# Rotating queries and keys on chip instead of by accumulating transfers

## The chip, the cores and the metric

The kernel runs on one core of a Trainium2 chip. The core has five engines that matter here: PE (TensorE, matrix products), DVE (VectorE), ACT (ScalarE), POOL (GpSimd) and SP (SyncE). Each takes its instructions strictly in the order in which they stand in its own program. PE, DVE and ACT compute; SP issues plain transfers; POOL issues nothing but transfers that add into their destination. All transfers are carried out by 16 DMA engines that the two issuers share. The metric is the device time of one execution in microseconds (us), and the median of several runs is compared.

## The reference

One encoder layer is applied to two sequences, a sample of 1024 tokens and a prompt of 512, with model width 2048. One input projection feeds a convolution group and an attention group of 8 query heads over 2 key and value heads. This work is about one step of it, the rotary embedding of queries and keys:

```python
def apply_rope(t, pos):
    half = HEAD_DIM // 2
    ...
    t1, t2 = tf[..., :half], tf[..., half:]
    out = jnp.concatenate([t1 * cos - t2 * sin, t2 * cos + t1 * sin], axis=-1)

def mixer_layer(x, ...):
    h = rms_norm(x, norm_g)
    z = h @ w_in
    c_val, c_glu, c_gate, q, k, v, a_gate = jnp.split(z, split_points, axis=-1)
    q = apply_rope(q.reshape(B, S, N_HEADS, HEAD_DIM), pos)
    k = apply_rope(k.reshape(B, S, N_KV_HEADS, HEAD_DIM), pos)
    ...
    return x + jnp.concatenate([conv_out, attn_out], axis=-1) @ w_out
```

The head dimension is 128. On the chip a head is stored transposed: the 128 dimensions lie on the 128 partitions and 512 tokens lie along each partition. The halves t1 and t2 are then partitions 0 to 63 and 64 to 127, and an elementwise engine operation does not bring a value from one half to the other unless its output is placed on other partitions than its input.

## The kernel before

**Products in units.** Each float32 operand is split into a high and a low part, and a product of blocks is three matmuls. The sample's projection goes in units: a unit computes two columns of outputs (c = 0, 1) for two halves of the tokens (t = 0, 1) with seven block products P1, P2, P6, P5, P7, P3, P4 of 12 matmuls each, in that order, with sums and differences of the operands (`Unit.product`, L177). The products accumulate in three PSUM banks that PE reuses inside the unit: P1, P6, P7 and P4 follow each other in bank `a`, P5 and P3 in bank `c`, P2 is in `b`. After P1, P6, P5, P7 and P4 the bank's content is copied out by ACT before the next product goes on adding to it (`Unit.tap`, L217); DVE adds the pieces (L237).

**Preparing weights.** For a unit, DVE forms differences of weight blocks (L138), ACT rounds each block to its high part (L438), and DVE forms the low part (L439). The same two engines also carry the taps, the convolution (DVE, L906, one of 31 taps at a time) and the attention.

**Totals.** Each unit runs over half of the inner dimension; the second pass over a column pair adds the first pass's result, which lies in DRAM (`part_q` for queries, `part_kv` for keys and values, `part_gate`, `part_conv`). That addition is an accumulating transfer issued by POOL (`add_into`, L429). What is to be done with a total is a generator that goes into a list; it takes its first step some products later (`turn_over`; `landing` = 4) and one further step at each product after that.

**The rotation.** For queries and keys that step is `rotate` (sample, in units) or `rotated` (prompt, whose jobs leave a complete result in a PSUM bank). DVE multiplies the result once by the table of sines (L932, into a second tile `b`) and once by the table of cosines (L933); SP stores the cosine product to DRAM (`q_d`, `k_d`); POOL then issues two accumulating transfers, which add the two halves of `b` crosswise into what was stored. In the sample the second tile comes from a ring of four tiles named `a`. Attention reads `q_d` and `k_d` from DRAM later.

**What sets the order.** The program is written out once; each engine's order is fixed by a scheduler that estimates times. Tiles come from rings of fixed length: whoever takes a tile waits until the last user of that place in the ring has finished. At the end of the sample's projection (`last_before`, L1719) SP loads the prompt's 16 input blocks (`xr_d`, L1709 into ring `a`, L1706 into ring `p`), and ACT and DVE split each into two parts (L441, L442) between the taps of the last unit.

Of the kernel before, what the change touches and what calls it, by code (L numbers as in the profile page):

```python
# [9 lines left out]
AF = mybir.ActivationFunctionType  # L10
ALU = mybir.AluOpType
PSUM = bass.MemoryType.PSUM

P = 128
# [19 lines left out]
W = 512  # L34
# [619 lines left out]
class Sequence:  # L654
# [270 lines left out]
            nc.vector.tensor_tensor(self.cos, self.cos, self.R, ALU.mult)  # L925
            nc.vector.tensor_tensor(self.sin, self.sin, self.R, ALU.mult)

    def rope(self, acc, c, o, b):

        nc = self.e.nc  # L930
        i = slice(c * W, c * W + W)
        nc.vector.tensor_tensor(b, acc, self.sin[:, i], ALU.mult)  # L932
        nc.vector.tensor_tensor(o, acc, self.cos[:, i], ALU.mult)  # L933

    def rotated(self, dst, accs):
        e = self.e
        o, b = e.G(), e.E()
        self.rope(accs[0], 0, o, b)
        self.put_rotated(dst, o, b)

    def put_rotated(self, dst, o, b):
        e, half = self.e, P // 2
        e.store(dst, o)
        e.add_into(dst[0:half], b[half:])
        e.add_into(dst[half:], b[0:half])

    def rotate(self, dst):
        def done(t, z):
            b = self.e.A([W], F32)
            self.rope(z, t, z, b)  # L950
            self.put_rotated(dst[:, t * W : t * W + W], z, b)
            yield

        return done
# [902 lines left out]
```

## Time and profile before

| | |
|---|---|
| three runs | 2134.34, 2138.23, 2139.43 us; median 2138.23 us |
| profiled execution, first to last instruction | 2137.4 us |
| time of the profiled execution outside that span | not shown; the span lies among the times of the runs |
| busy: PE, DVE, ACT, POOL | 2085.0, 1668.7, 1063.8, 156.6 us |
| PE without work | 2137.4 - 2085.0 = 52.4 us |
| transfers issued by SP, by POOL | 431.99 MB, 39.33 MB |
| rotations | 20 in the sample (645 to 841 us), 10 in the prompt (891 to 1047 us) |

A row of the timeline gives the start and the duration in us, the engine, the line of the kernel, the operation, what it writes and reads (buffer numbers left out) and a count; in square brackets stands how long the engine had been idle before it and what ended that idle time. A row of waits gives the engine and the waiting line, what it waited for, the total, the number of times and the longest. A row of stretches gives the span in us and then for PE, PEld (weight load), DVE, ACT and POOL the busy time, the granted PE clock as a share of full speed, the DMA share and GB/s. "SPq" and "POOLq" are transfers issued there.

### The profile page before, as it was taken

Reading aid. Unit: us, or ns where it says so; the run is one execution under the profiler, and the core shown is the slowest. Engines: PE = TensorE matmul, PEld = TensorE weight load, DVE = VectorE, ACT = ScalarE, POOL = GpSimd, SP = SyncE. Lnnn points to the kernel's source line nnn. Section 1 sums busy time; section 2 is a strip of 40 time slices with the busy share of each in tenths; the row PEclk is TensorE's granted clock in tenths of the full one; section 3 lists DMA queues with packets and bytes.
Section 4 is the critical chain, followed back from the end, with each engine's and each line's share of the span. In section 5 each row is a group of like instructions: output and inputs, shape, how many; then the busy total and the mean of one; then the engine's idle time right before and its main releaser. Section 6 shows DMA issues by size and latency. Waiting matters only on the chain. (4 is left out here: it accounts for less than half of the span.)

```text
span 2137.4 us, 26915 instructions
## 1 busy us (share of the span) xinstructions
PE 2085.0 (98%) x9330; PEld 1711.9 (80%) x9330; DVE 1668.7 (78%) x2551; ACT 1063.8 (50%) x1736; POOL 156.6 (7%) x184
## 2 busy tenths in 40 slices
PE   8999999999999999899999999999999989999998
PEld 7878888888888787688888888878888867887886
DVE  8757899988898788888887786668799667887543
ACT  7475436333554344554556776235545464563232
POOL 0001110000013233001000000000000001110000
PEclk9999999999999999999999999999999999999999
DMA  8888878854768888966664546886766369799952
GB/s 288 306 286 246 229 178 266 279 179 157 232 179 184 198 178 222 279 176 174 168 213 161 197 158 227 317 298 232 256 237 206 107 209 267 188 299 314 306 177 79
DMA packets 241209, 473.04 MB, mean 221 GB/s; under 512 B 23088, under 2 KB 80816, under 8 KB 241072
## 3 DMA queue, kind: packets, MB, share of 16 engines
q1 hardware_dynamic: 218992, 431.99, 60.5%
q0 software_dynamic: 22080, 39.33, 11.6%
q8 instruction: 73, 1.20, 0.2%
q14 instruction: 64, 0.52, 0.1%
HBM read 319.19 MB, written 152.04 MB: 220 GB/s over the span
## 5 line engine op out<-in xcount | busy, mean ns | idle before, releaser
L191 PE MATMUL a<-t,hl 128*128 128x512 f32 x2640 | 636.6, 392 | 22.5 <-ACT u L217 12.3
L191 PEld LDWEIGHTS a<-t,hl 128*128 128x128 f32 x2640 | 495.5, 189 | 132.8 <-ACT u L217 16.4
L438 ACT ACTIVATE hl<-raw 128x1024 fp32r<-128x1024 f32 (+1 forms) x330 | 296.2, 898 | 376.9 <-DVE raw L138 82.8
L439 DVE TENSOR_TENSOR hl<-raw,hl 128x1024 fp32r<-128x1024 f32 (+1 forms) x330 | 338.4, 1026 | 182.3 <-ACT hl L438 180.4
L906 DVE SCALAR_TENSOR_TENSOR f<-f,c_w_dw,f 128x1024 f32<-128x1024 f32 (+1 forms) x464 | 456.5, 1014 | 0.0
L578 PE MATMUL a<-t,hl 128*128 128x512 f32 x1344 | 328.9, 394 | 2.2 <-DVE f L848 2.2
L191 PE MATMUL c<-t,hl 128*128 128x512 f32 x1320 | 320.1, 390 | 1.6 <-ACT g L217 0.9
L578 PEld LDWEIGHTS a<-t,hl 128*128 128x128 f32 x1344 | 249.1, 188 | 53.0 <-DVE f L848 2.6
L191 PEld LDWEIGHTS c<-t,hl 128*128 128x128 f32 x1320 | 247.6, 188 | 53.8 <-ACT g L217 1.5
L578 PE MATMUL c<-t,hl 128*128 128x512 f32 x672 | 168.1, 397 | 0.0
L578 PE MATMUL b<-t,hl 128*128 128x512 f32 x672 | 162.6, 392 | 0.8 <-DVE hl L439 0.8
L191 PE MATMUL b<-t,hl 128*128 128x512 f32 x660 | 161.1, 390 | 0.0
L578 PEld LDWEIGHTS b<-t,hl 128*128 128x128 f32 x672 | 125.2, 188 | 26.1 <-DVE hl L439 1.2
L578 PEld LDWEIGHTS c<-t,hl 128*128 128x128 f32 x672 | 124.8, 189 | 24.4
L191 PEld LDWEIGHTS b<-t,hl 128*128 128x128 f32 x660 | 123.5, 188 | 25.1
L217 ACT ACTIVATE u<-a 128x512 f32<-128x512 f32 x114 | 67.2, 592 | 75.4 <-PE a L191 64.0
L217 ACT ACTIVATE g<-a 128x512 f32<-128x512 f32 x106 | 62.8, 592 | 76.8 <-PE a L191 70.3
L1540 PE MATMUL a<-hl,t 128*128 128x512 f32 x192 | 74.3, 390 | 0.0
L346 ACT ACTIVATE hl<-raw 128x1024 fp32r<-128x1024 f32 x44 | 46.4, 1054 | 46.7 <-PE b L578 15.2
L429 POOL DMA_DIRECT2D u<-part_out x16 | 14.0, 890 | 756.5 <-DVE t L439 697.4
L1044 ACT ACTIVATE p<-p,tiny 128x384 f32<-128x384 f32 (+1 forms) x96 | 54.5, 569 | 29.6 <-DVE tiny L1041 21.1
L438 ACT ACTIVATE a<-pt 128x512 fp32r<-128x512 f32 x64 | 38.0, 594 | 59.4 <-PE pt L1064 59.3
(312 smaller groups left out, 2581.2 us busy)
## 6 DMA issues: line engine op xcount, KB each, us to landing
raw<-w_in SPq DMA_DIRECT2D x171, 512.0 KB, 5.3
raw<-w_out SPq DMA_DIRECT2D x64, 256.0 KB, 4.5
raw<-w_out SPq DMA_DIRECT2D x31, 512.0 KB, 4.6
raw<-w_pw SPq DMA_DIRECT2D x24, 512.0 KB, 5.1
p<-xT_s SPq DMA_DIRECT2D x40, 256.0 KB, 5.3
f<-x_s SPq DMA_DIRECT2D x16, 512.0 KB, 7.2
f<-y_d SPq DMA_DIRECT2D x16, 512.0 KB, 5.9
y_s<-f SPq DMA_DIRECT2D x16, 512.0 KB, 4.6
```

Of the source, the lines that this page charges most:

```text
L191: nc.tensor.matmul(acc, hl[:, l, o, j, :], toks[j][:, r], start=name in FRESH and j == 0 and q == 0, stop=name in LAST and j == HALF - 1 a ...
L217: nc.scalar.activation(t, bank, AF.Copy)
L346: e.nc.scalar.activation(t[:, 0], raw, AF.Copy)
L429: self.nc.gpsimd.dma_start(dst, src, accum_op=ALU.add)
L438: nc.scalar.activation(hi, x, AF.Copy)
L439: nc.vector.tensor_tensor(lo, x, hi.bitcast(F32), ALU.subtract)
L578: nc.tensor.matmul(job.acc[0], hl[:, l, kk // HALF, kk % HALF, :], r, start=i == 0 and p == 0, stop=i == nk - 1 and p == 2,)
L906: nc.vector.scalar_tensor_tensor(t, h[:, j : j + T], w(j), t, ALU.mult, ALU.add)
L1044: nc.scalar.activation(p[:, 0:n], p[:, 0:n], AF.Exp, bias=nm[:, h : h + 1], accum_out=l[:, h : h + 1])
L1540: nc.tensor.matmul(acc, self.mix[self.KS[i]][:, m, b * P : (b + 1) * P], part[l].rearrange("p a b -> p (a b)"), start=i == 0 and p == 0, s ...
```

## The change

ACT copies the result's halves crosswise into the second tile (two copies of 64 partitions x 512), DVE multiplies the result by the cosines, the copy by the sines, and adds the two, and SP stores the sum once. The two accumulating transfers of each rotation are gone. The table of sines changes the sign of its halves. In the sample the generator has one more step: the copies come where the two multiplications were, the DVE work one product later.

```diff
-    def rope(self, acc, c, o, b):
+    def exchanged(self, b, x):
+
+        half = P // 2
+        self.e.nc.scalar.activation(b[half:], x[0:half], AF.Copy)
+        self.e.nc.scalar.activation(b[0:half], x[half:], AF.Copy)
+
+    def rope(self, dst, o, b, x, c):
 
         nc = self.e.nc
         i = slice(c * W, c * W + W)
-        nc.vector.tensor_tensor(b, acc, self.sin[:, i], ALU.mult)
-        nc.vector.tensor_tensor(o, acc, self.cos[:, i], ALU.mult)
+        nc.vector.tensor_tensor(o, x, self.cos[:, i], ALU.mult)
+        nc.vector.tensor_tensor(b, b, self.sin[:, i], ALU.mult)
+        nc.vector.tensor_tensor(o, o, b, ALU.add)
+        self.e.store(dst, o)
 
     def rotated(self, dst, accs):
         e = self.e
         o, b = e.G(), e.E()
-        self.rope(accs[0], 0, o, b)
-        self.put_rotated(dst, o, b)
-
-    def put_rotated(self, dst, o, b):
-        e, half = self.e, P // 2
-        e.store(dst, o)
-        e.add_into(dst[0:half], b[half:])
-        e.add_into(dst[half:], b[0:half])
+        self.exchanged(b, accs[0])
+        self.rope(dst, o, b, accs[0], 0)
 
     def rotate(self, dst):
         def done(t, z):
             b = self.e.A([W], F32)
-            self.rope(z, t, z, b)
-            self.put_rotated(dst[:, t * W : t * W + W], z, b)
+            self.exchanged(b, z)
+            yield
+            self.rope(dst[:, t * W : t * W + W], z, b, z, t)
             yield
...
-    arrays["sin"] = np.concatenate([sin, -sin])
+    arrays["sin"] = np.concatenate([-sin, sin])
```

In the changed kernel the copies are L931 and L932, the three DVE operations L938, L939 and L940, and the loads of `xr_d` are L1712 and L1709.

Three places show what this moves. In the waits, DMASW is a semaphore of POOL's transfers, DMAHW one of SP's.

POOL, among the query units of the sample. Before, each pair of additions into `q_d` stands between the additions of `part_q`:

```order
L429 DMA g_6787<-part_q_01_399 128x512
L429 DMA q_d_1_109<-a_6831 64x512 x2
L429 DMA u_6876<-part_q_10_400 128x512
L429 DMA g_6899<-part_q_00_404 128x512
L429 DMA q_d_1_109<-a_6940 64x512 x2
L429 DMA u_6976<-part_q_11_407 128x512
```

In the changed kernel:

```order
L429 DMA g_6802<-part_q_01_399 128x512
L429 DMA u_6893<-part_q_10_400 128x512
L429 DMA g_6916<-part_q_00_404 128x512
L429 DMA u_6994<-part_q_11_407 128x512
L429 DMA u_6953<-part_q_01_405 128x512
```

Only the totals are left, one behind the other; over the whole program POOL has 60 transfers fewer.

SP, at the end of the sample's projection, where the prompt's inputs `xr_d` are loaded. Before, three of the four first loads into ring `a` wait for POOL's transfers:

```order
L1709 DMA a_7166<-xr_d_0_186 128x1024 [waits DMASW5_49,DMAHW3_49,DMASW4_49,DMASW3_49]
L432 DMA ag_d_7_103<-u_6936 128x512 [waits DMAHW4_49,Activation_49]
L432 DMA q_d_1_109<-g_7025 128x512 [waits DMAHW5_49,DVE_49]
L1709 DMA a_7168<-xr_d_1_187 128x1024 [waits DMAHW6_49,DMASW7_49,DMASW0_49]
L1709 DMA a_7170<-xr_d_2_188 128x1024 [waits DMAHW7_49,DMASW5_49,DMASW4_49]
L896 DMA f_7408<-h_d_5_85 128x1024 [waits DMAHW0_49]
L1706 DMA p_7174<-xr_d_4_190 128x512 [waits DMAHW1_49]
L1709 DMA a_7172<-xr_d_3_189 128x1024 [waits DMAHW2_49,DMASW7_49,DMASW0_49]
L432 DMA gate_d_4_92<-u_7047 128x512 [waits DMAHW3_49,Activation_49]
```

In the changed kernel:

```order
L1712 DMA a_7186<-xr_d_0_186 128x1024 [waits DMAHW4_49]
L1712 DMA a_7188<-xr_d_1_187 128x1024 [waits DMAHW5_49]
L1712 DMA a_7190<-xr_d_2_188 128x1024 [waits DMAHW6_49]
L896 DMA f_7428<-h_d_5_85 128x1024 [waits DMAHW7_49,DVE_49]
L432 DMA q_d_1_109<-g_7044 128x512 [waits DMAHW0_49,DVE_49]
L1712 DMA a_7192<-xr_d_3_189 128x1024 [waits DMAHW1_49,Activation_49]
L1709 DMA p_7194<-xr_d_4_190 128x512 [waits DMAHW2_49]
L432 DMA gate_d_4_92<-u_7066 128x512 [waits DMAHW3_49,Activation_49]
```

The waits on POOL's transfers are gone from the loads; the last rotation's store, which waits for DVE's sum, now stands behind the third load and ahead of the fourth.

ACT, in one query unit of the sample, from the tap of P6 to the tap of P4 (taps are L217, weights L438, L888 is the gate's activation). Before:

```order
L217 ACTIVATE u_6342<-a_6279 128x512 [waits DMAHW7_49,PE_49]
L888 ACTIVATE g_6194<-g_6194 128x512 [waits DVE_49]
L217 ACTIVATE g_6364<-c_6338 128x512 [waits DMAHW0_49,PE_49]
L438 ACTIVATE hl_6366<-raw_6267 128x1024 [waits DMAHW6_49,Activation_49]
L217 ACTIVATE u_6382<-a_6279 128x512 [waits PE_49]
L438 ACTIVATE hl_6410<-raw_6267 128x512 [waits DVE_49,PE_49,Activation_49]
L438 ACTIVATE hl_6410<-p_6406 128x512 [waits DVE_49]
L217 ACTIVATE g_6431<-a_6279 128x512 [waits DMAHW3_49,PE_49,Activation_49]
```

In the changed kernel:

```order
L217 ACTIVATE u_6652<-a_6588 128x512 [waits DMAHW3_49,PE_49]
L931 ACTIVATE a_6656<-u_6592 64x512 [waits DMASW3_49]
L888 ACTIVATE g_6501<-g_6501 128x512 [waits DVE_49]
L932 ACTIVATE a_6656<-u_6592 64x512
L217 ACTIVATE g_6671<-c_6648 128x512 [waits DMAHW4_49,PE_49]
L438 ACTIVATE hl_6673<-raw_6573 128x1024 [waits DMAHW2_49,Activation_49]
L217 ACTIVATE u_6693<-a_6588 128x512 [waits PE_49]
L931 ACTIVATE a_6697<-g_6615 64x512 [waits DMASW4_49]
L932 ACTIVATE a_6697<-g_6615 64x512
L438 ACTIVATE hl_6718<-raw_6573 128x512 [waits DVE_49,PE_49,Activation_49]
L438 ACTIVATE hl_6718<-p_6714 128x512 [waits DVE_49]
L217 ACTIVATE g_6743<-a_6588 128x512 [waits DMAHW7_49,PE_49,Activation_49]
```

Two pairs of copies have come between the same taps, and the first copy of each pair waits for a total that a transfer of POOL brings.

## The prediction

> **What bounds the kernel now.** I read the page's totals first, then the stretches, then the waits of PE, then the timeline at the largest gaps.
>
> ```profile
> PE 2085.0 (98%) x9330; PEld 1711.9 (80%) x9330; DVE 1668.7 (78%) x2551; ACT 1063.8 (50%) x1736; POOL 156.6 (7%) x184
> 200.00:650.00 450.00, 450.00 (x1987) 372.74 (x1986) 403.24 (x526) 205.91 (x314) 34.30 (x40) 1.00 0.71 212
> 640.00:850.00 210.00, 203.04 (x895) 165.75 (x894) 168.02 (x226) 84.36 (x131) 69.08 (x80) 1.00 0.84 195
> 850.00:890.00 40.00, 31.58 (x126) 24.11 (x125) 29.16 (x42) 23.72 (x37) 6.77 (x8) 0.91 0.97 292
> 890.00:1060.00 170.00, 168.09 (x790) 137.57 (x790) 148.21 (x220) 82.71 (x154) 16.79 (x20) 1.00 0.67 182
> 873.00:906.00 33.00, 28.17 (x126) 22.30 (x125) 28.10 (x41) 16.69 (x27) 4.22 (x5) 1.00 0.90 261
> ```
>
> PE is busy 98% of the span, and the change leaves its matmuls alone. So only PE's idle time and its slow clock can be won, and work on the other engines costs something only where PE waits for it. From 200 to 650 us, units without rotation, PE has no gap at all although DVE is 403.24 / 450 = 90% busy. In the stretch with the sample's rotations (640 to 850) it lacks 210 - 203.04 = 7.0 us, in the next 40 us it lacks 8.4 and the clock falls to 0.91, in the prompt's rotations (890 to 1060) it lacks 1.9. That is where to look.
>
> First the large gap. SP's own waits, then the timeline:
>
> ```profile
> SPq L1709 <- DMA q_d<-a: 10.1, 2, 9.5
> 843.41 0.49 SPq L1706 DMA_DIRECT2D p<-xr_d  x1
> 848.92 1.68 POOL L429 DMA_DIRECT2D q_d<-a  x2 [9.96 <-DVE raw L138]
> 854.06 0.32 SPq L1709 DMA_DIRECT2D a<-xr_d  x1
> 860.67 1.33 ACT L441 ACTIVATE t<-a,c_norm_g 128x512 fp32r<-128x512 f32 x2 [5.67 <-DMA a<-xr_d]
> 863.65 0.57 ACT L217 ACTIVATE u<-a 128x512 f32<-128x512 f32 x1
> 864.28 4.68 PE L191 MATMUL a<-t,hl 128*128 128x512 f32 x12 [5.34 <-ACT u L217]
> 868.81 2.90 PE L191 MATMUL c<-t,hl 128*128 128x512 f32 x12
> 860.00:865.00 5.00, 0.72 (x2) 0.63 (x3) 5.00 (x8) 4.33 (x8) 0.88 (x1) 0.61 1.04 401
> ```
>
> Read it backwards. PE waits 5.34 us for a tap. ACT gives the tap late because a split of a prompt block (L441) stands ahead of it and waits 5.67 us for its load. SP issues that load only at 854.06, after 9.5 us in which it waits for the last rotation's second tile; and that tile is held until POOL's two additions, issued from 848.92, have landed. After the gap the 12 matmuls run at a low clock.
>
> Now the small gaps between 640 and 850:
>
> ```profile
> 839.43 2.88 PE L191 MATMUL a<-t,hl 128*128 128x512 f32 x12
> 842.15 2.88 PE L191 MATMUL c<-t,hl 128*128 128x512 f32 x12
> 686.67 0.60 ACT L217 ACTIVATE u<-a 128x512 f32<-128x512 f32 x1 [0.59 <-PE a L191]
> 687.84 0.32 SPq L432 DMA_DIRECT2D q_d<-u  x1
> 693.10 1.68 POOL L429 DMA_DIRECT2D q_d<-a  x2 [3.42 <-DMA q_d<-u]
> 694.29 1.42 POOL L429 DMA_DIRECT2D u<-part_q  x1
> 704.34 0.69 DVE L932 TENSOR_TENSOR a<-u,f 128x512 f32<-128x512 f32 x1 [8.04 <-issue]
> 708.02 2.57 PE L191 MATMUL a<-t,hl 128*128 128x512 f32 x10 [1.33 <-DVE hl L439]
> 715.73 3.02 PE L191 MATMUL a<-t,hl 128*128 128x512 f32 x12 [2.43 <-ACT u L217]
> DVE a L932 <- issue: 17.8, 5, 8.0
> DVE a L932 <- DMA g<-part_kv: 7.1, 2, 6.7
> ```
>
> A product takes 842.15 - 839.43 = 2.72 us. At 686.67 a tap leaves a piece whose total POOL should fetch, but POOL stands before the additions into `q_d`, which wait for a store issued at 687.84; the total is issued at 694.29, and DVE's rotation waits for it until 704.34. Weights and taps behind it come late: 1.33 and 2.43 us on PE. Such waits of the rotation sum to 17.8 + 7.1 us and more.
>
> **The change, part by part.** Prices:
>
> ```profile
> L429 POOL DMA_DIRECT2D q_d<-a x32 | 28.2, 1000 | 89.6 <-DVE u L237 21.9 <-DVE raw L138 19.0 <-DVE a L932 17.2
> L933 DVE TENSOR_TENSOR u<-u,f 128x512 f32<-128x512 f32 x10 | 6.9, 688 | 0.1
> L888 ACT ACTIVATE u<-u 128x512 f32<-128x512 f32 x16 | 10.1, 630 | 20.1 <-DVE u L882 20.1
> L438 ACT ACTIVATE hl<-raw 128x1024 fp32r<-128x1024 f32 x208 | 219.5, 1056 | 211.0 <-PE a L578 33.2 <-issue 30.1 <-DVE raw L138 26.2
> q0 software_dynamic: 8944, 15.73, 48.2%
> u<-part_q POOLq DMA_DIRECT2D x16, 256.0 KB, 7.0
> u<-part_conv POOLq DMA_DIRECT2D x14, 256.0 KB, 5.5
> ```
>
> *Removed:* 60 transfers of about 1.0 us on POOL (the order shows them gone, so the change does what it says), 40 of them between 640 and 850 us. There POOL's queue carries 15.73 MB in 48.2% of the DMA engines' time, and 40 x 131 KB = 5.2 MB of it go. Totals then go out right behind their taps, and should land in 5.5 us, as `part_conv` does from 200 to 350 us, rather than 7.0 (medians of the two stretches).
>
> *Added on DVE:* one sum per rotation, 0.69 us. In the sample 20 x 0.69 = 13.8, so (168.0 + 13.8) / 210 = 87% busy, under the 90% at which PE had no gap; it is hidden by the waits of 17.8 + 7.1 us that go. In the prompt 10 x 0.69 = 6.9: (148.2 + 6.9) / 170 = 91%, with little cover.
>
> *Added on ACT:* 60 copies of 64 x 512. No row has 64 partitions. Bounds: half of 0.63 = 0.32 and the full 0.63; 128 x 1024 takes 1.06, so time follows the elements along a partition, and I take 0.63. That is 1.26 us per rotation; the sample's stretch goes to (84.4 + 25.2) / 210 = 52%. The Trainium skill (ScalarE: Activation LUTs, section "What ACT_TABLE_LOAD costs") speaks against splitting a tile so: an ACTIVATE costs a fixed 186 ns plus 0.833 ns per element of a partition. By it two halves would cost 2 x 0.61 us, by plain area 0.63; the path's sum would be the same while cover lasts.
>
> Does it last? What is queued behind a copy that waits is the next tap, and PE waits for that. I count one unit from P1's end in steps of 2.72. P6 ends at 5.4 and its tap (0.6, after 0.2) at 6.2; the first pair of copies and the gate take 1.9, to 8.1; P5 ends at 8.2, its tap at 9.0, and P3 needs it at 10.9. So the first pair has some 2 us to spare, and the total it waits for was tapped three products earlier, 8.2 us, against 5.5 to 7.0 for landing. The second pair, behind P7's tap (11.7), ends at 13.0; P4 is tapped from 16.5. The next P1's tap stands behind a rounding (L438, 1.06) that waits for DVE's last difference (L138): P3 ends at 13.6, six DVE operations at a pace of 0.6 follow, so 17.2 and 18.3; two of the three new operations come in between, 1.2, so 19.5; the tap is needed by 21.8. That leaves 21.8 - 0.6 - 19.5 = 1.7 us, enough unless DVE waits longer. If the cover were gone, each pair would cost 1.26 us on PE.
>
> *Moved, sample:* the gaps of 7.0 us (between all kept and none) become, I take, 1.0: **-6.0**.
>
> ```profile
> 840.57 0.69 DVE L933 TENSOR_TENSOR g<-g,f 128x512 f32<-128x512 f32 x1
> 878.84 0.69 DVE L882 TENSOR_TENSOR u<-u,f 128x512 f32<-128x512 f32 x1 [2.79 <-DMA u<-part_gate]
> 889.72 5.94 PE L578 MATMUL a<-t,hl 128*128 128x512 f32 x25 [2.18 <-DVE f L848]
> ```
>
> *Moved, SP:* the store of the last rotation needs DVE's sum. The cosine product was at 840.6 and the rotation moves by one product (2.7), plus one sum: about 844 to 845, so the fourth load goes out at 845 rather than 854. ACT then splits blocks from about 851 on without a stop; eight splits of 1.33 / 2 = 0.67 end near 857, the tap by 857.5, and PE needs it at 864.28 - 5.34 = 858.9. Gain: the gap 5.34 and the slow clock (868.81 - 864.28) - 2.72 = 1.81. What is late next is the other loads and the gate totals in the same rush, with 1.4 us to spare: 0 to 3 us new, 1.0 taken. **-6.1.**
>
> The Trainium skill (TensorE: Matmul & The Clock Gate, Part 1) says the clock halves after an idle window of about 3.4 us. By it a leftover gap under 3.4 us costs only itself; the trace agrees, a clock of 0.61 after 5.34 us, and 12 matmuls in 3.02 us after the gap of 2.43.
>
> *Start of the prompt (873 to 906):* 33 - 28.17 = 4.8 us idle, from gate totals that DVE waits for (2.79) and weights that come late behind them (2.18), none of which the change touches: 0. Earlier loads may clear it, a changed order may add the like of one more such gap: -4.8 to +3.
>
> *Prompt:* the reads of the finished bank go from DVE to ACT, where exponentials and weights queue behind a copy that waits for PE's last matmul; PE's order there was written for estimated times. Bounds: at best the 1.9 us idle there go, at worst all copies show, 10 x 1.26 = 12.6; ACT at (82.7 + 12.6) / 170 = 56% lies nearer to nothing, DVE at 91% does not: **+1.0**.
>
> Sum: -6.0 - 6.1 + 1.0 = -11.1, so 2126.3 us against the profiled 2137.4. That execution lies 0.8 below the median 2138.23, which gives **2127 us**, -0.5%.
>
> **The rivals.** (a) *Only one stall goes.* The small gaps stay since taps still stand behind DVE's differences, or the fourth load meets another wait. For it: DMA share 0.97 in 850 to 890. Against: SP's row names one culprit. 2138.2 - 6.1 = 2132. (b) *More goes.* With the loads 9 us earlier the rush is over before the prompt starts and its 4.8 us vanish too: 2127 - 5 = 2122; for it, DVE works at 873 to 906 on splits left over. (c) *The prompt takes it back:* copies that wait for PE hold up the exponentials, half of 12.6 or more: 2127 + 8 = 2135. (d) *Slower:* ACT's copies stand in front of taps in the sample and wait there for totals. It decides once a total lands later than some 2 us past its turn, or slack is under 1.26 us: 20 x 1.26 = 25 us on PE, 2138.2 - 6.1 + 25 = 2157. Against: 8.2 us for landing, ACT 52% busy.
>
> **How the numbers follow.** Forecast 0.50 (alone 2122.5 to 2131.5), (a) 0.18, (b) 0.15, (c) 0.10, (d) 0.07. Range 2119 to 2136: from (b) with some more to (c); only (d) and tails lie outside. A measurement here can tell about 0.3%, 6.4 us: faster means under 2131.8. Nearly all of the forecast, (b) and a third of (a) are that: 0.70; the rest of (a) and (c), 0.22; slower, (d) and a little, 0.08.
>
> **What would show it.** Right: SP's wait on `q_d<-a` absent, the fourth load near 845, no PE gap over 3 us around 860 and a clock of 1.00 there; PE's stretch of the sample's rotations within 2 us of full; POOL's totals landing near 5.5; copies of 0.6 us. Wrong: PE waiting for L217 behind L931, copies of 0.3 us, new gaps from 890 to 1060, or the same 5 us gap with another releaser.

## The result and the profile after

The changed kernel takes 2127.0 us (median of four runs, 2124.1 to 2130.9) beside 2138.8 us for the kernel before (four runs, 2134.3 to 2141.1). The ratio is 0.9939, 95% interval 0.9921 to 0.9957: faster by 0.6%. The profiled execution has a span of 2122.5 us and a time of 2124.3 us.

The page's totals and the stretches of the changed kernel, in the columns of the stretches before:

```profile
PE 2083.2 (98%) x9330; PEld 1713.7 (81%) x9330; DVE 1683.2 (79%) x2581; ACT 1102.5 (52%) x1796; POOL 104.8 (5%) x124
640.00:850.00 210.00, 210.00 (x936) 173.91 (x935) 185.93 (x257) 120.47 (x184) 38.26 (x44) 1.00 0.76 187
840.00:880.00 40.00, 35.01 (x151) 27.91 (x150) 32.33 (x46) 28.05 (x43) 4.36 (x5) 1.00 0.96 296
858.00:891.00 33.00, 27.66 (x125) 22.09 (x124) 28.32 (x43) 16.86 (x22) 2.62 (x3) 1.00 0.85 268
880.00:1050.00 170.00, 168.09 (x790) 138.22 (x789) 155.70 (x230) 94.31 (x176) 0.00 (x0) 1.00 0.51 166
```

From 640 to 850 us, the sample's rotations, PE has no gap left (7.0 us before). In the 40 us behind, PE lacks 5.0 us at full clock (8.4 us at 0.91 before), at the prompt's start (858 to 891, the same work as 873 to 906 before) 5.3 (4.8 before), and in the prompt's rotations 1.9, as before. The work on DVE and ACT in the first of these stretches has grown by 17.9 and 36.1 us (185.93 - 168.02, 120.47 - 84.36), and PE doesn't feel it; part of the growth is work that the program, which is ahead, now reaches within the same stretch.

The timeline of the changed kernel at the end of the sample, SP's loads first, then the split, the tap and every gap of PE from 600 to 880 us:

```profile
829.93 2.26 SPq L1712 DMA_DIRECT2D a<-xr_d  x3
836.93 0.38 SPq L1712 DMA_DIRECT2D a<-xr_d  x1
855.08 1.33 ACT L441 ACTIVATE t<-a,c_norm_g 128x512 fp32r<-128x512 f32 x2 [2.05 <-DMA a<-xr_d]
856.95 3.02 PE L191 MATMUL a<-t,hl 128*128 128x512 f32 x12 [1.29 <-ACT u L217]
861.94 10.78 PE L578 MATMUL b<-t,hl 128*128 128x512 f32 x46 [1.52 <-DVE hl L439]
875.36 5.97 PE L578 MATMUL a<-t,hl 128*128 128x512 f32 x25 [2.18 <-DVE hl L439]
```

The fourth load goes out at 836.93 in a program that is 8.5 us ahead by then (the product that started at 844.88 starts at 836.38), the gap of 5.34 us with the slow clock behind it is gone (the product behind it, now at 849.99, follows without a gap), and what is left is three gaps of 1.3 to 2.2 us. The new operations and the totals, by groups of one line each (the first three rows: nanoseconds at least, median and at most) and by the transfers from 640 to 850 us (the fourth: number, size, median us from issue to landing; the last, POOL's queue: packets, MB and share of the DMA engines' time):

```profile
L931 ACT ACTIVATE a<-u x10: 630/632/635, 645.3 to 810.0; 64x512 f32<-64x512 f32 x10
L931 ACT ACTIVATE u<-b x3: 588/588/592, 874.2 to 990.0; 64x512 f32<-64x512 f32 x3
L940 DVE TENSOR_TENSOR u<-u,a x10: 678/683/686, 650.9 to 816.8; 128x512 f32<-128x512 f32 x10
u<-part_q POOLq DMA_DIRECT2D x16, 256.0 KB, 4.9
q0 software_dynamic: 6336, 11.54, 35.1%
```

**A finer measure.** Executions of one kernel differ by 7 us among four here, and by 18 in one set of 20 of the kernel before, so a time alone can't tell two changed kernels apart. One stretch of the trace leaves out what differs ahead of it and behind it: from POOL's first total of the kv units (the first row of each pair) to PE's first matmul of the prompt (the second).

Kernel before:

```profile
637.13 0.86 POOL L429 DMA_DIRECT2D u<-part_kv  x1 [6.05 <-DMA gate_d<-g]
874.74 0.61 PE L578 MATMUL b<-t,hl 128*128 128x512 f32 x2
```

Changed kernel:

```profile
637.08 0.87 POOL L429 DMA_DIRECT2D u<-part_kv  x1 [6.29 <-DMA gate_d<-g]
859.81 0.61 PE L578 MATMUL b<-t,hl 128*128 128x512 f32 x2
```

That is 237.6 us before and 222.7 after, 14.9 us less. From there to the last matmul's row it takes 1250.15 us before and 1250.20 after. So the whole difference between these two profiles lies in this stretch, and the prompt's half of the change shows neither gain nor cost. All kernels of the experiments, in this measure, with the ratio of their times to the kernel before:

| kernel | stretch, us | ratio (95% interval) |
|---|---|---|
| before | 237.6 | |
| changed | 222.7 | 0.9939 (0.9921 to 0.9957) |
| `e1_last_tile` | 239.3 | 0.9994 (0.9979 to 1.0008) |
| `e5_free_loads` | 240.3 | 1.0009 (0.9996 to 1.0022) |
| `e2_totals_first` | 228.5 | 0.9945 (0.9924 to 0.9966) |
| `e12_both` | 225.3 | 0.9951 (0.9933 to 0.9969) |
| `e6_both_free` | 228.4 | 0.9947 (0.9931 to 0.9962) |
| `e7_last_four_on_chip` | 230.6 | 0.9955 (0.9940 to 0.9970) |
| `e9_first_late_last_on_chip` | 224.1 | 0.9920 (0.9906 to 0.9934) |
| `e3_dummy_adds` | 223.3 | 0.9934 (0.9920 to 0.9948) |
| `e4_double_copies` | 230.1 | 0.9954 (0.9938 to 0.9969) |
| `e8_sample_only` | 222.2 | 0.9931 (0.9915 to 0.9947) |
| `e10_other_ring` | 220.4 | 0.9927 (0.9912 to 0.9942) |

The stretch comes from one profile of each kernel, and POOL's total is not tied to PE's products. Counted from the start of a PE product ahead of it instead (618.91 us before, 619.53 after), the change gives 15.6 us, and the others' differences to the kernel before move by at most 1.3 us. So stretches that lie closer than some 1.5 us can't be told apart.

### The profile page after: what moved, and what is told of

Read it like the earlier page. It is cut to its first block, busy times and chain, and to the rows that moved or that the text cites. A ratio compares the mean times of both kernels' runs of the same rounds, so it can differ in the third digit from the quotient of the medians.

```text
span 2122.5 us, 26858 instructions
## 1 busy us (share of the span) xinstructions
PE 2083.2 (98%) x9330; PEld 1713.7 (81%) x9330; DVE 1683.2 (79%) x2581; ACT 1102.5 (52%) x1796; POOL 104.8 (5%) x124
## 4 chain that ended last, share of the span: by engine, by line
PE 82%; DMA 6%; issue 5%; DVE 4%; ACT 2%; POOL 1%; SPq 0%; ACTq 0%; POOLq 0%; DVEq 0%
PE a L191 23%; PE a L578 12%; PE c L191 11%; PE c L578 7%; PE b L191 6%; PE b L578 6%; PE s L191 2%; PE s L1033 2%; PE a L1543 2%; PE s L1543 2%; PE pv L1062 2%; DMA f<-x_s 1%; PE pt L1067 1%; PE pt L191 1%; PE pv L1543 1%
## 5 line engine op out<-in xcount | busy, mean ns | idle before, releaser
L438 ACT ACTIVATE hl<-raw 128x1024 fp32r<-128x1024 f32 (+1 forms) x330 | 296.4, 899 | 347.4 <-DVE raw L138 61.0
L217 ACT ACTIVATE u<-a 128x512 f32<-128x512 f32 x114 | 67.2, 591 | 79.3 <-PE a L191 67.3
L217 ACT ACTIVATE g<-a 128x512 f32<-128x512 f32 x106 | 62.9, 594 | 81.1 <-PE a L191 68.5
L439 DVE TENSOR_TENSOR a<-pt,a 128x512 fp32r<-128x512 f32 x64 | 43.9, 686 | 29.6 <-ACT a L438 29.4
L438 ACT ACTIVATE a<-pt 128x512 fp32r<-128x512 f32 x64 | 38.1, 595 | 55.6 <-PE pt L1067 55.4
L346 ACT ACTIVATE hl<-raw 128x1024 fp32r<-128x1024 f32 x44 | 46.3, 1053 | 31.8 <-DMA raw<-w_in 11.8
```

The costliest lines, as they stand in the source:

```text
L217: nc.scalar.activation(t, bank, AF.Copy)
L346: e.nc.scalar.activation(t[:, 0], raw, AF.Copy)
L438: nc.scalar.activation(hi, x, AF.Copy)
L439: nc.vector.tensor_tensor(lo, x, hi.bitcast(F32), ALU.subtract)
```

## The experiments

**SP's wait alone: two runs, no gain.** The first takes the second tile of the sample's last rotation from another ring:

```diff
+            self.turned = getattr(self, "turned", 0) + 1
-            b = self.e.A([W], F32)
+            b = self.e.A([W], F32) if self.turned < 20 else (self.e.G, self.e.U)[t]()
```

> The kernel before, with one edit: the second tile of the sample's last rotation comes from another ring, so the prompt's fourth load no longer needs a tile that the last additions hold. All 60 additions and their order on POOL stay. Theory (two separate waits): the large gap goes alone. SP has no wait of 9.5 us on additions into q_d, the gap of 5.34 us near 860 and the low clock behind it are gone or under 2 us, while 640 to 850 us keeps about 7 us of PE idle time; 2138.8 - 6 = 2133 us (2130 to 2135). Rival A (the additions' bytes crowd the DMA engines): the loads still land late, the gap near 860 stays at 4 us or more, 2137 to 2140 us.

The time didn't move. The timeline of this kernel shows where the wait went:

```profile
832.05 0.45 SPq L123 DMA_DIRECT2D raw<-w_in  x1
840.49 0.32 SPq L1710 DMA_DIRECT2D a<-xr_d  x1
840.91 0.38 SPq L432 DMA_DIRECT2D ag_d<-u  x1
845.29 0.60 ACT L217 ACTIVATE u<-c 128x512 f32<-128x512 f32 x1 [8.03 <-DMA ag_d<-u]
845.94 4.35 PE L191 MATMUL c<-t,hl 128*128 128x512 f32 x12 [5.03 <-ACT u L217]
863.46 0.63 ACT L888 ACTIVATE g<-g 128x512 f32<-128x512 f32 x1 [3.44 <-DVE g L882]
865.86 4.61 PE L191 MATMUL a<-t,hl 128*128 128x512 f32 x12 [1.97 <-ACT u L217]
```

The scheduler, which thinks the tile free sooner, has put the load earlier. SP now stands 8 us before it (832.5 to 840.49) for the tile of the rotation before; a store waits behind it, a tap waits for the store's tile, and PE has its 5 us gap at 846 instead of 864. At 866 a gap of 1.97 us is left, again with a slow clock: there ACT waits 3.44 us for a gate product of DVE, with the tap behind it. So the first run moved the wait and did not test it. The second frees all four tiles (the last four rotations use places that are long free) and holds the loads back until then:

```diff
-        e.store(dst, o)
+        self.stored = getattr(self, "stored", []) + [e.nc.sync.dma_start(dst, o)]
...
-            b = self.e.A([W], F32)
+            self.turned = getattr(self, "turned", 0) + 1
+            b = self.e.A([W], F32) if self.turned < 17 else self.e.PT("p", NP, [W]) if self.turned < 19 else (self.e.G, self.e.U)[t]()
...
-        for j in range(0, 12, 2):
-            load_two(j)
+        with e.tc.issue_after(sample.stored[-2].ins):
+            for j in range(0, 12, 2):
+                load_two(j)
```

> The kernel before, POOL's order untouched: the second tiles of the sample's last four rotations come from other rings, and the prompt's first loads are queued on SP behind the store of the last rotation but one, so all four A tiles are free when SP comes to them and no load waits for an addition, here or earlier. Theory (the stall of the first of these runs was only moved forward; a real removal is worth its gap and slow clock): no SP wait over 3 us between 820 and 860, no PE gap over 3 us near 860, 640 to 850 us keeps 5 to 7 us idle, 2139 - 6 = 2133 us (2130 to 2135). Rival D (the fourth load never set the end: the rush of splits and totals on DVE behind it takes over at once): a PE gap of 4 us or more near 860 stays, 2136 to 2140 us.

Its timeline, SP, then POOL, DVE, ACT and PE:

```profile
826.45 2.15 SPq L1710 DMA_DIRECT2D a<-xr_d  x4
850.29 1.68 POOL L429 DMA_DIRECT2D q_d<-u  x2 [9.62 <-DVE raw L138]
851.42 2.38 POOL L429 DMA_DIRECT2D g<-part_gate  x2
860.41 0.69 DVE L882 TENSOR_TENSOR g<-g,f 128x512 f32<-128x512 f32 x1 [5.81 <-DMA g<-part_gate]
864.39 0.63 ACT L888 ACTIVATE g<-g 128x512 f32<-128x512 f32 x1 [7.07 <-DVE g L882]
866.77 4.81 PE L191 MATMUL a<-t,hl 128*128 128x512 f32 x12 [5.59 <-ACT u L217]
```

All four loads go out together at 826.45 and none waits. The gap is still there, 5.59 us with a slow clock behind it, and rival D is right for this kernel. (Two gaps of 1.85 and 1.30 us are new, at 838.77 and 844.58, in the rush of these loads; they account for the longer stretch.) Its rows give the chain: POOL's last additions stand ahead of two gate totals; DVE waits 5.81 us for such a total with the splits queued behind; ACT's next operation waits 7.07 us for DVE, and the tap stands behind it. So two chains end at that tap, one through SP's load and one through the gate totals, and both begin at the same additions. Taking away the first alone is worth nothing.

**POOL's order alone: nearly two thirds of the gain, by the stretch.** Every transfer stays, but the sample's additions are queued behind the totals of their unit:

```diff
-            e.add_into(d, part)
+            i = e.nc.gpsimd.dma_start(d, part, accum_op=ALU.add)
+            with e.tc.issue_after(i.ins if hasattr(i, "ins") else i):
+                while e.held_adds and n[1] == 0:
+                    e.held_adds.pop(0)()
...
+            d, half = dst[:, t * W : t * W + W], P // 2
             self.rope(z, t, z, b)
-            self.put_rotated(dst[:, t * W : t * W + W], z, b)
+            self.e.store(d, z)
+            self.e.held_adds.append(lambda: self.e.add_into(d[0:half], b[half:]))
+            self.e.held_adds.append(lambda: self.e.add_into(d[half:], b[0:half]))
```

> The kernel before, with one edit: the sample's additions are queued on POOL behind the totals of their unit instead of ahead of them, so a total no longer stands behind an addition that waits for a store. Every transfer and every byte stays, and so does the wait of SP's fourth load, since the tile is held even longer. Theory: the small gaps go alone. 640 to 850 us has under 2 us of PE idle time (7.0 before), the rotation's multiplications wait for no total for 8 us, the gap near 860 stays at 5 us or more; 2138.8 - 6 = 2133 us (2130 to 2136). Rival A (bytes): the totals land as late as before, 640 to 850 us keeps 5 to 7 us idle, 2137 to 2140 us.

The stretch of the rotations, then SP, ACT and PE at its end:

```profile
640.00:850.00 210.00, 209.36 (x931) 172.95 (x930) 174.92 (x234) 89.95 (x138) 71.81 (x83) 1.00 0.88 209
848.90 0.32 SPq L1715 DMA_DIRECT2D a<-xr_d  x1
854.37 0.72 ACT L444 ACTIVATE t<-a,c_norm_g 128x512 fp32r<-128x512 f32 x1 [2.90 <-DMA a<-xr_d]
855.62 5.49 PE L191 MATMUL a<-t,hl 128*128 128x512 f32 x12 [4.32 <-ACT u L217]
```

PE's idle time from 640 to 850 us falls from 7.0 to 0.6, with the DMA engines busier than before (0.88, then 0.84). The stretch is 9.2 us shorter and the time 11 us (0.9945), more than the 6 expected of it; no bytes were saved. By its time this kernel can't be told from the changed one, so how the gain divides rests on the profiles. At the end the gap stays, 4.32 us, a little under the 5 expected. Here ACT does wait for the fourth load (2.90), and that wait ends last, since the gate totals go out at 836.85 and 839.87 instead of 850.06: of the two chains, the other one is now last.

**Both waits.** One run joins the first edit to the totals-first kernel, another joins the second.

> The kernel before with both edits: additions behind the totals of their unit, and the last rotation's second tile from another ring. All 60 accumulating transfers stay, no copy and no sum is added. Theory: both waits gone, nearly the whole gain without taking a transfer away: under 2 us idle from 640 to 850, no gap over 3 us near 860, 2125 to 2129 us. Rival A (bytes): 2135 us or more. Rival B (the change won by the order that its other instructions took, not by the two waits): 2133 us or more.

> The run with the totals first, and its four A tiles free as in the run before. Both waits gone, all transfers kept. Theory (two waits, each worth its gaps): lower than the totals-first run by the gap near 860, about 5 us: 2122 to 2125 us; from the first total of the kv units to the prompt's first matmul 223 to 225 us (228.5 totals first, 222.7 changed kernel). Rival D: no lower than the totals-first run, 2126 to 2129 us.

By its time (2129.0 us) the first is at the upper end of what was expected, but 2.3 us of idle time are left from 640 to 850 us, in one gap before a tap that waits 5.94 us for the tile of a store of `ag_d`, as in the first run; by its stretch (225.3) it lacks 2.6 us to the changed kernel. At the end the gap is down to 0.73 us. Rival B is out all the same: it takes nearly the whole gain with nothing but the two waits changed. The second is no better than the totals alone, in time (2131.6 us) or stretch; 2122 to 2125 and 223 to 225 were expected. Its ACT and PE:

```profile
836.23 0.60 ACT L217 ACTIVATE u<-c 128x512 f32<-128x512 f32 x1 [5.99 <-DMA ag_d<-u]
836.88 3.03 PE L191 MATMUL c<-t,hl 128*128 128x512 f32 x12 [2.62 <-ACT u L217]
855.54 4.54 PE L191 MATMUL a<-t,hl 128*128 128x512 f32 x12 [2.03 <-ACT u L217]
```

With four loads of 512 KB issued in a row from 819.40 on, the DMA engines are full from there, two stores of `ag_d` need 8.7 to 9.1 us to land, and a tap waits 5.99 us for the tile of one. This edit has a new gap of 2.62 us, and 2.03 us with a slow clock are left at the end, so the run does not settle what freeing both is worth. The next pair goes another way.

**By rotation instead of by wait.** Two kernels do only the last four of the sample's rotations on chip (two copies, two products, a difference, one store); the first sixteen keep their additions, in the old order or behind the totals.

```diff
+            if self.turned > 16:
+                nc, half, i = self.e.nc, P // 2, slice(t * W, t * W + W)
+                nc.scalar.activation(b[half:], z[0:half], AF.Copy)
+                nc.scalar.activation(b[0:half], z[half:], AF.Copy)
+                yield
+                nc.vector.tensor_tensor(z, z, self.cos[:, i], ALU.mult)
+                nc.vector.tensor_tensor(b, b, self.sin[:, i], ALU.mult)
+                nc.vector.tensor_tensor(z, z, b, ALU.subtract)
+                self.e.store(dst[:, i], z)
+                yield
+                return
```

> The kernel before, with only the sample's last four rotations done on chip (two copies, two products, one difference, one store); the first sixteen keep their additions in the old order. Theory as the runs so far have changed it (one wait, POOL's order: at the end the last additions stand ahead of the gate totals, so DVE's splits and the tap behind them are late; SP's wait was not what set the gap): the gap near 860 and its slow clock go, under 3 us there, the gaps of the first sixteen rotations stay (5 to 6 us up to 800 us), and from the kv units' first total to the prompt's first matmul it takes 229 to 231 us (237.6 before, 228.5 totals first, 222.7 changed). Time about 8 us below the kernel before. Rival F (the small delays of all rotations add up and the end only shows them): the gap near 860 stays above 4 us, 233 us or more.

> The totals-first kernel, with the last four of the sample's rotations on chip: 32 of the sample's 40 additions stay, behind the totals; no addition stands near the gate totals or holds a tile that the prompt's loads need. Theory: all of the change's gain, 222 to 225 us from the kv units' first total to the prompt's first matmul, within 3 us of the changed kernel in time. Rival (the gap of 4 to 7 us between the totals-first and the changed kernel belongs to all rotations): 227 us or more.

Every PE gap over 0.2 us between 640 and 864 us of the first of them, by its timeline:

```profile
705.40 2.56 PE L191 MATMUL a<-t,hl 128*128 128x512 f32 x10 [0.28 <-DVE hl L439]
713.11 4.60 PE L191 MATMUL a<-t,hl 128*128 128x512 f32 x12 [2.43 <-ACT u L217]
792.16 3.04 PE L191 MATMUL a<-t,hl 128*128 128x512 f32 x12 [1.00 <-ACT u L217]
856.01 3.04 PE L191 MATMUL a<-t,hl 128*128 128x512 f32 x12 [0.97 <-ACT u L217]
862.88 3.06 PE L191 MATMUL a<-t,hl 128*128 128x512 f32 x12 [1.06 <-ACT u L217]
```

The large gap is down to 0.97 and 1.06 us; the gaps of the first sixteen rotations stay, though smaller than expected (3.7 us instead of 5 to 6). With the totals first as well, the stretch is 224.1 us, 1.4 from the changed kernel, while 32 of the sample's 40 additions are still made. The pieces of the gain, in the stretch: 7.0 us for the last four rotations (237.6 - 230.6), 6.5 for the order of POOL in the first sixteen (230.6 - 224.1), 1.4 for the rest (8.3, 6.2 and 1.1 counted from the PE product). The last piece is no larger than what this measure can tell. Rival F and the other rival are out. By its time the second is 17 us below the kernel before (0.9920) and the changed one 12, where they were expected within 3 of each other; the intervals overlap.

**Bytes.** The changed kernel gets 40 accumulating transfers back among the sample's totals, of the old size, from an input table into memory that nobody reads, so that they wait for nothing and nobody waits for them:

```diff
+            d, half = self.waste[self.wasted], P // 2
+            with self.e.tc.issue_after(self.e.last_total):
+                self.e.add_into(d[0:half], self.e.a["cos"][half:, 0:W])
+                self.e.add_into(d[half:], self.e.a["cos"][0:half, 0:W])
```

> The changed kernel with 40 accumulating transfers put back between the sample's totals on POOL, of the same size and in places like those of the old additions, but from an input table into memory that nobody reads, so none of them waits for anything and nobody waits for it. Theory (waits, not bytes): within 3 us of the changed kernel, 2125 to 2130 us, under 2 us of PE idle time from 640 to 850. Rival A (bytes and POOL's issue time): the totals land late again, 5 us or more idle from 640 to 850, 2133 us or more.

Its stretch, the landing of its totals, POOL's queue, and some rows of POOL's timeline:

```profile
640.00:850.00 210.00, 210.00 (x935) 173.83 (x934) 186.21 (x257) 119.88 (x182) 71.67 (x84) 1.00 0.91 211
u<-part_q POOLq DMA_DIRECT2D x16, 256.0 KB, 5.2
q0 software_dynamic: 9536, 16.78, 50.1%
675.46 0.86 POOL L245 DMA_DIRECT2D u<-part_q  x1 [5.45 <-DVE u L237]
676.00 1.97 POOL L429 DMA_DIRECT2D waste_d<-cos  x2
683.55 0.88 POOL L245 DMA_DIRECT2D g<-part_q  x1 [5.58 <-DVE g L237]
```

POOL is as busy as before, its queue carries 16.78 MB, and PE has no gap. The totals land in 5.2 us as against 4.9 without these bytes. So neither the bytes nor POOL's issue time were what the additions cost; what is left is the wait for the store, with totals queued behind it. Rival A is out. One thing differs besides the wait: the old additions stood right ahead of a total, these mostly stand right behind one, so what additions without a wait would cost right ahead of a total was not run.

**Copies and prompt.** Each copy done twice, and the prompt's rotations left as they were:

```diff
-        self.e.nc.scalar.activation(b[half:], x[0:half], AF.Copy)
-        self.e.nc.scalar.activation(b[0:half], x[half:], AF.Copy)
+        for _ in range(2):
+            self.e.nc.scalar.activation(b[half:], x[0:half], AF.Copy)
+            self.e.nc.scalar.activation(b[0:half], x[half:], AF.Copy)
```

> The changed kernel, with each crosswise copy done twice: 60 more copies of 0.63 us, 1.26 us more per rotation on ScalarE. Theory (slack of 1.7 to 2.0 us counted at the taps in the sample): 640 to 850 us keeps under 2 us of PE idle time and the time stays within 3 us of 2127, at most 2130. Rival C (the copies stand just at the limit of their cover): each further pair shows on PE, 20 x 1.26 = 25 us in the sample, 2152 us, or 2140 if half of them show; in the prompt 10 x 1.26 = 12.6 us at worst.

> The changed kernel, with the prompt's ten rotations done as before (a store and two additions, no copies and no sum; the sign of the sine is put into the product). Theory: the prompt's part of the change is neutral, 2125 to 2130 us, and the time from the prompt's first matmul to the last one within 2 us of 1250.2 us. Rival E (the prompt pays for its copies and the sample gives more than was measured): 2122 us or less, or (the prompt gives part of the gain) 2131 us or more.

The kernel with double copies, its stretch, SP's first three loads and the gap at the end:

```profile
640.00:850.00 210.00, 208.17 (x922) 170.94 (x921) 181.21 (x250) 139.61 (x219) 37.40 (x43) 1.00 0.73 179
833.02 2.92 SPq L1713 DMA_DIRECT2D a<-xr_d  x3
861.64 4.33 PE L191 MATMUL a<-t,hl 128*128 128x512 f32 x12 [3.05 <-ACT u L217]
```

Among the rotations 1.8 us of the 25.2 added on ACT show on PE, in three gaps of 0.5 to 0.7 us; at these three places the slack is used up. At the end the loads start 3.1 us later (833.02 for 829.93) and a gap of 3.05 us opens with a slow clock, so the stretch grows by 7.3 us in all. The time, 2128.1 us, shows less of that than the profile (0.9954, an interval that overlaps the changed kernel's). In the prompt ten more pairs cost nothing that can be seen: 1251.3 us from its first matmul to the last, 1250.2 without.

With the prompt's additions kept, the stretch is 222.2 us and the time 2128.1 us (0.9931), as with the whole change: the gain is the sample's. The time behind the stretch, 1254.4 us, misses the 2 us that I allowed, but kernels whose prompt is done as before spread from 1246.8 (`e9_first_late_last_on_chip`) to 1255.1 us (`e7_last_four_on_chip`) there; what the prompt's part is worth inside some 4 us can't be told.

**What is left.** One edit on the changed kernel, from the wait of 2.05 us in its profile: the prompt's last two loads use the ring of the rotation's tables.

```diff
-        t = e.A([2, TP], F32)
+        t = e.F([2, TP]) if j >= 12 else e.A([2, TP], F32)
```

> The changed kernel, with the prompt's last two loads taken into the ring of the rotation's tables in place of the A ring, so that they go out some 8 us earlier or more. Theory: the wait of 2.05 us of ACT's split for that load is gone and with it the PE gap of 1.29 us near 857; the gaps behind it (1.5 and 2.2 us, weights behind splits on DVE) stay: 221 to 222 us from the kv units' first total to the prompt's first matmul (222.7 changed), 1 to 2 us below the changed kernel, which the times can't tell from nothing.

From 640 to 870 us this kernel's PE has one gap:

```profile
859.47 11.16 PE L578 MATMUL b<-t,hl 128*128 128x512 f32 x46 [1.40 <-DVE hl L439]
```

The stretch is 220.4 us, the shortest of all, 2.3 under the changed kernel and a little under the 221 to 222 expected. Its time is 2124.9 us against 2141.3 before in the same set (0.9927); the interval overlaps the changed kernel's, so it beats the kernel before for certain and the changed one by its profile only.

## Why the prediction held, step by step

**The time.** 2127 us was forecast and 2127.0 measured. The sum was 11.1 us, the medians differ by 11.8, and the two profiles by 14.9. That the forecast and the median agree to a few tenths is luck: four executions of the changed kernel spread over 6.8 us. Against the traces the terms came out a little small. Of the 14.9 us, 11.0 are idle time of PE (7.0 + 5.3 before, 1.3 after) and 1.8 the slow clock behind the large gap. Most of the rest lies in the products beside a gap, which take 2.85 to 2.88 us instead of 2.72 (by the starts in the trace): the forecast priced a gap by the idle time in its row alone. It also set the span of the profiled execution, 2137.4, beside whole times, though a time is longer than its span (2124.3 and 2122.5 in the changed kernel); with 11.1 us taken off the median this changes nothing.

**Small gaps in the sample, -6.0: right, and the mechanism too.** 7.0 us went where 6.0 were taken. That POOL's additions wait for the store with totals queued behind is shown: moving them behind the totals removes 6.3 of the 7.0 us (`e2_totals_first`), and putting transfers back that do not wait returns none of it (`e3_dummy_adds`). A part of my reasoning was only company: totals that land sooner (4.9 us, where I took 5.5) would have come with the bytes or without (5.2).

**The SP stall, -6.1: right in size, with half of its cause.** The step read one chain back from the gap, SP's fourth load and the tile, and stopped there ("SP's row names one culprit"). The load did go out where I put it (836.93, some 845 in the old program's time, for 845), and no load waits for an addition into `q_d` any more. But loads freed in another way gained nothing (`e5_free_loads`; the other run moved the wait). A second chain hangs from the same additions, through POOL's queue to the gate totals, DVE and ACT, and ends at the same tap. I had it under "what is late next" with 0 to 3 us; taken alone it keeps the whole 5.6. The trace of the kernel before holds it too:

```profile
850.06 2.37 POOL L429 DMA_DIRECT2D g<-part_gate  x2
860.02 0.69 DVE L882 TENSOR_TENSOR g<-g,f 128x512 f32<-128x512 f32 x1
861.91 0.61 ACT L888 ACTIVATE g<-g 128x512 f32<-128x512 f32 x1
```

The two gate totals go out right behind the additions of 848.92, and DVE's second product ends at 860.71, when ACT has waited for its load until 860.67: the chains end within 0.1 us of each other, and ACT has both operations ahead of the tap. The change was worth its 7 us there because it takes away the common root of both. Rival (a), "the fourth load meets another wait", is what an edit to the loads alone would have met.

**What is late next, 1.0 us: small.** The tap that the step computes ends at 849.77, and PE goes on at 849.99 without a gap: 0.2 us to spare, not 1.4. What is late next is the tap behind it, which waits for the last loads (a gap of 1.29 us, 0.14 before); doubling the copies opens it to 3.05, and `e10_other_ring` closes it.

**The start of the prompt, 0: nearly.** 4.8 us of idle time became 5.3, a gap of 1.52 us where 0.75 were before and one of 1.64 for 1.90; so rival (b), in which they vanish, did not come.

**The prompt, +1.0: nothing.** From its first matmul to the last it took 0.05 us more, inside what this part can tell; rival (c) is out, even with double copies.

**Prices.** 0.63 us for a copy of 64 partitions was taken and 0.632 measured from SBUF (0.588 from PSUM), and 128 partitions take 0.630 (L888), so halving the partitions saves nothing; 0.69 for the sum, 0.683 measured. DVE is at 89% in the rotations for the forecast 87, ACT at 57% for 52.

**Slack.** I counted 2 us before the first pair of copies and 1.7 at the last tap. With 1.26 us more per pair nearly all rotations still hide it, so the slack is 1.26 us or more at nearly all of them. At the three that show 0.5 to 0.7 us it is, by estimate, 0.6 to 0.8 (1.26 less the gap), about 1 us under my count. Rival (d), 25 us, did not come even with twice the copies.

## What to carry to other kernels

A transfer that has to wait is paid by what stands behind it in its queue, so look there before you count its bytes: 40 transfers of the same size cost 0.6 us of the stretch, no more than it can tell, when they wait for nothing, and the old ones some 9 of its 15 by waiting ahead of others. When a gap's chain has been followed back to a culprit, ask which other chains reach the same gap from the same root; an edit that cuts one of them gains little or nothing, and one that removes the root gains nearly all. And measure such a change in the stretch that it touches, since whole times of this program spread by 7 us and more.

## What the runs showed of the hardware

The slow clock follows shorter gaps than I had read from the trace of before, where 12 matmuls behind a gap of 2.43 us took 3.02 us. In two other kernels:

```profile
838.77 4.51 PE L191 MATMUL a<-t,hl 128*128 128x512 f32 x12 [1.85 <-ACT g L217]
838.00:844.00 6.00, 4.51 (x12) 3.03 (x12) 5.02 (x7) 1.42 (x4) 0.90 (x1) 0.72 1.07 280
```

This is `e5_free_loads`: a gap of 1.85 us, then a granted clock of 0.72 over 6 us, and 12 matmuls take 4.51 us. In `e7_last_four_on_chip` the same gap of 2.43 us as before, quoted above, is followed by 4.60 us. The Trainium skill (TensorE: Matmul & The Clock Gate, Part 1) names an idle window of about 3.4 us for the slow clock and calls the window free-running. Here single gaps of 1.85 and 2.43 us were enough in some executions, while gaps of 2.43 (the kernel before) and 2.62 us (`e6_both_free`, 3.03 us behind it) were not in others. The measurement decides: the forecast's rule that a gap under 3.4 us costs only itself does not hold, and a gap of 2 us may cost nearly 2 us more.

A plain store can land late among loads. In the kernel before, the last rotation's store goes out at 841.29, among 512 KB loads, and lands 7.1 us later, where such stores take 3.4 to 3.6 us (medians from 640 to 850 us); the additions that need it are issued at 848.92. That the loads are the cause is not shown by a run.
